# A hybrid GLA and Fourier encoder layer: exponentials behind an eviction, x in four pieces, gated state steps, gate loads by chunk

## The chip, the cores and the metric

The kernel runs on one core of one Trainium2 chip. The metric is the device time of one execution in microseconds; the time before is the median of three runs. A profiled execution gives the rows below. Engines are named as in the rows: PE is TensorE, DVE is VectorE, ACT is ScalarE, POOL is GpSimd, SP is SyncE, which issues nearly all DMAs.

## What is computed

One encoder layer in float32, 2048 positions by 1024 features:

```python
proj = x @ w_in                                  # q k v gates z_gla u z_fnet, 2592 wide
log_a = log_sigmoid(gate_lowrank @ w_up + b) / 16  # one per direction
o = gla_forward(q, k, v, log_af) + gla_backward(q, k, v, log_ab)   # 4 heads
y_gla = rmsnorm(o) * g * silu(z_gla)
y_fnet = (fft2(u, over positions and group features).real @ w_fnet) * silu(z_fnet)
y = concat(y_gla, y_fnet) @ w_out
out = layernorm(2 ** 0.25 * x + y) * ln_g + ln_b
```

`gla` is a scan: a state of 64x128 per head is decayed by exp(log_a) and receives k^T v at each position.

## The kernel before

Products keep nearly full float32 accuracy by splitting every operand into a rounded part ("hi", a copy by ScalarE at L55) and a remainder ("lo", a subtraction by DVE at L58); each product is three matmuls, hi*hi, hi*lo, lo*hi. The function `split` does both, so these two lines stand for many tiles (`xhl`, `bhl`, `et`, `yhl`, `mix`, `shl`, `wA_w`), and rows are told apart by tile.

The program has four phases. Phase 1 projects x to z_gla, u and z_fnet. Phase 2 merges two generators on TensorE: `qk_all`, which projects x to q and k in 8 blocks of 256 positions (L86, 96 matmuls a block), and `fnet_pe`, the Fourier part by groups g = 0 to 3: an FFT of 16 points over position blocks in DVE operations on `fw` (L522 to L534), its operands `bhl`, matmuls with the table `et` (`stage2`, L635), `yhl`, and `mixdown` (L655 into two buffers `pg`, a copy `qs`, and DVE's sum and difference L661 and L662). The first steps, the warm-up, are q and k blocks alone.

Phase 3 goes over 8 blocks of 256: projections pw and pv (L94), the gates' low-rank part (`gate_evac`, L781 to L783, evicts `rn`; `gate_t` transposes it at L813 and copies R at L814), the gate matmuls L825, `gates1` (scans L843 and L845), `gates2` with `middle` (L866 and the clip L867), and `gates3` (exponentials L872 and L873, `scaled` at L891 and L892, `alphas` L947 to L953). Each block also does the GLA chunks of the block before: `gla_s` and `gla_m` (scores L905, L906, transposes L909, masks L917, L918) and `gla_b` (the states' additions, L928, evicted to S by L930 and L932, and the inner part L935, evicted to `oi` by L939). GpSimd chains the states in `chain_step`: an addition L1194 and a multiplication with alpha L1197.

A handover (b = NBLK) does the last block's GLA part while the first output chunks start and the output weight is loaded; `find_range` checks the size of the exponents and writes a flag with a small matmul, L1063. Phase 4 goes over 16 chunks of 128 positions from 15 down to 0: `prep` (loads, a backward state step on GpSimd, the state matmul L1268, L1273, a square and its split), `norm` (L1282, L1283, scaling, and the multiplication with the gate z at L1289, on DVE for chunks 15 to 13 and on GpSimd below), `outp` (L1220, weights `wB` for the Fourier half and `wA` for the GLA half) and `finish` (residual, layer norm, store; L1299 to L1319).

Instructions are recorded in program order and then ordered by a scheduler of the language, engine by engine, by its own model of times. `tc.issue_after(ins)` adds one constraint: what is recorded inside stands behind `ins` wherever it runs on the engine of `ins`; `after(...)` in phase 3 joins several.

## Time and profile before

| | |
|---|---|
| time, median of 3 runs | 787.35 us (787.26 to 787.60) |
| profiled execution | 788.25 us, span of instructions 786.5 us |
| TensorE (PE) | 748.6 us busy, 95%, 5254 matmuls |
| DVE | 549.8 us, 70% |
| ScalarE (ACT) | 381.1 us, 48% |
| GpSimd (POOL) | 196.5 us, 25% |
| granted clock of TensorE, mean | 0.995 of full |
| DMA | 130.75 MB, mean 166 GB/s |

The profiled execution's span lies 1.75 us below its own time. "Idle before" in a row is the time for which the engine did nothing ahead of the instruction, with what released it. A row of the timeline can join several instructions (x4); a duration includes a pipeline's tail, so that starts of neighbours lie closer than durations.

### The profile page before, as it was taken

The numbers are of one execution on the slowest core, as the hardware profiler recorded it, in microseconds if no ns is written. First come the engines' busy times: TensorE is split into PE (matmuls) and PEld (weight loads), VectorE is DVE, ScalarE is ACT, GpSimd is POOL, SyncE is SP. The second block draws the span as 40 slices with busy tenths as digits, with TensorE's granted clock in tenths as the row PEclk, the third lists the DMA queues.
The fourth block names the chain that finished last, engine by engine and source line by source line (L and its number), as shares of the span: only waits on it lengthen the run. The fifth ranks groups of instructions, "written<-read, shape, count | busy, mean of one in ns | idle before, by whom it ended". The sixth has DMA issues, their size and how long they took to land.

```text
span 786.5 us, 13529 instructions
## 1 busy us (share of the span) xinstructions
PE 748.6 (95%) x5254; PEld 691.2 (88%) x5254; DVE 549.8 (70%) x808; ACT 381.1 (48%) x707; POOL 196.5 (25%) x137
## 2 busy tenths in 40 slices
PE   6999999999999998989999989999998999999995
PEld 5988899999999998989999888889876788888884
DVE  4693467464545789895748888888868777776764
ACT  6674372233223453445546777776655334334341
POOL 0000003020211000213310414444454454544531
PEclk9999999999999999999999999999999999999998
DMA  8876352444126974555775664555455454444222
GB/s 244 267 210 186 118 192 72 150 114 140 68 94 179 272 239 164 156 168 190 239 214 163 185 184 156 154 166 158 139 175 219 168 184 165 166 144 172 108 81 85
DMA packets 81935, 130.75 MB, mean 166 GB/s; under 512 B 7523, under 2 KB 55651, under 8 KB 81862
## 3 DMA queue, kind: packets, MB, share of 16 engines
q1 hardware_dynamic: 79558, 125.60, 50.5%
q10 hardware_dynamic: 2304, 4.20, 1.5%
q8 instruction: 43, 0.70, 0.4%
q14 instruction: 30, 0.25, 0.1%
HBM read 93.07 MB, written 36.70 MB: 165 GB/s over the span
## 4 chain that ended last, share of the span: by engine, by line
PE 55%; DVE 21%; ACT 11%; DMA 8%; issue 3%; SPq 1%; POOL 0%; DVEq 0%; ACTq 0%
PE mm L1220 17%; PE mm L374 17%; PE mm L86 4%; DMA xraw<-in_xt_dram 3%; DVE c L845 3%; PE mm L291 3%; PE mm L94 2%; DVE c L843 2%; ACT xhl L55 2%; DVE fw L534 2%; PE pa L635 2%; DMA fw<-u_d 2%; DVE fw L531 1%; PE pg L291 1%; PE pa L291 1%
## 5 line engine op out<-in xcount | busy, mean ns | idle before, releaser
L94 PE MATMUL mm<-wA_w,xhl 128*128 128x272 f32 x768 | 105.1, 292 | 0.0
L94 PEld LDWEIGHTS mm<-wA_w,xhl 128*128 128x128 f32 x768 | 98.6, 189 | 0.0
L86 PE MATMUL mm<-xhl,wC_w 128*128 128x256 f32 x768 | 96.0, 284 | 0.0
L86 PEld LDWEIGHTS mm<-xhl,wC_w 128*128 128x128 f32 x768 | 93.7, 192 | 0.5 <-issue 0.5
L1220 PE MATMUL mm<-wA_w,mix 128*128 128x512 f32 (+1 forms) x384 | 90.0, 384 | 1.5 <-ACT mix L55 1.1
L1220 PE MATMUL mm<-wB_w,mix 128*128 128x512 f32 (+1 forms) x384 | 89.3, 387 | 0.0
L1220 PEld LDWEIGHTS mm<-wA_w,mix 128*128 128x128 f32 x384 | 70.3, 188 | 16.6 <-ACT mix L55 1.5
L1194 POOL TENSOR_TENSOR S<-S 64x512 f32<-64x512 f32 x30 | 51.2, 1708 | 124.2 <-ACT S L930 121.2
L1220 PEld LDWEIGHTS mm<-wB_w,mix 128*128 128x128 f32 x384 | 69.5, 189 | 13.0
L58 DVE TENSOR_TENSOR xhl<-xraw,xhl 128x1024 fp32r<-128x1024 f32 (+1 forms) x52 | 57.5, 1111 | 29.8 <-ACT xhl L55 29.5
L55 ACT CAST xhl<-xraw 128x1024 fp32r<-128x1024 f32 (+1 forms) x52 | 49.3, 951 | 39.3 <-DMA xraw<-in_xt_dram 20.0
L55 ACT CAST x<-xraw 128x1024 fp32r<-128x1024 f32 x28 | 29.3, 1048 | 69.0 <-PE mm L374 54.9
L436 POOL TENSOR_TENSOR t<-t,t 128x512 f32<-128x512 f32 x7 | 10.9, 1557 | 190.4 <-ACT t L435 190.4
L1318 POOL TENSOR_TENSOR r<-r,lnb 128x1024 f32<-128x1024 f32 x15 | 35.7, 2383 | 89.5 <-issue 51.2
L58 DVE TENSOR_TENSOR x<-xraw,x 128x1024 fp32r<-128x1024 f32 x28 | 37.8, 1352 | 28.7 <-ACT x L55 28.7
L670 POOL TENSOR_TENSOR yf<-yf,zfl 128x256 f32<-128x256 f32 x24 | 20.9, 900 | 121.3 <-ACT yf L649 111.9
L1197 POOL TENSOR_TENSOR S<-S,alpha 64x512 f32<-64x512 f32 x30 | 48.6, 1620 | 2.4
L374 PE MATMUL mm<-wC_s,x 128*128 128x256 f32 x384 | 48.2, 283 | 0.0
L374 PEld LDWEIGHTS mm<-wC_s,x 128*128 128x128 f32 x384 | 47.1, 192 | 0.1
L291 PE MATMUL mm<-xhl,wA_w 128*128 128x512 f32 x192 | 43.9, 389 | 0.0
L291 PEld LDWEIGHTS mm<-xhl,wA_w 128*128 128x128 f32 x192 | 36.0, 188 | 7.4
L55 ACT CAST mix<-zg 128x512 fp32r<-128x512 f32 x15 | 9.3, 622 | 58.8 <-POOL zg L1289 56.0
(210 smaller groups left out, 1497.3 us busy)
## 6 DMA issues: line engine op xcount, KB each, us to landing
xraw<-in_xt_dram SPq DMA_DIRECT2D x48, 512.0 KB, 4.7
xr<-in_x_dram SPq DMA_DIRECT2D x16, 512.0 KB, 3.6
out_dram<-r SPq DMA_DIRECT2D x15, 512.0 KB, 2.7
xraw<-in_xt_dram SPq DMA_DIRECT2D x24, 256.0 KB, 4.7
zg_d<-zs SPq DMA_DIRECT2D x32, 128.0 KB, 3.7
u_d<-t SPq DMA_DIRECT2D x16, 256.0 KB, 3.2
zf_d<-t SPq DMA_DIRECT2D x16, 256.0 KB, 2.4
zfl<-zf_d SPq DMA_DIRECT2D x32, 128.0 KB, 3.4
```

The lines of the kernel that those rows point to most:

```text
L55: nc.scalar.copy(out=hi, in_=src)
L58: return (lo_eng or nc.vector).tensor_tensor(out=lo, in0=src, in1=f32(hi), op=ALU.subtract)
L86: mm = self.nc.tensor.matmul(ps, w[:, s, k, c0:c0 + P], x[:, m, k % 4, :], start=(k == 0 and i == 0), stop=(k == KB - 1 and i == 2))
L94: self.nc.tensor.matmul(ps, x[:, s, k % 4, t * P:(t + 1) * P], w[:, m, k, c0:c0 + cols], start=(k == 0 and i == 0), stop=(k == KB - 1 and ...
L291: nc.tensor.matmul(ps[c], self.wzg[:, s, 2 * q + kk, c * P:(c + 1) * P], x[:, m, kk], start=(q == 0 and kk == 0 and j == 0), stop=(q == 3 ...
L374: nc.tensor.matmul(ps[:, i], s_[s][:, k, i * P:(i + 1) * P], m_[m][:, k], start=(k == 0 and j == 0), stop=(k == 3 and j == 2))
L670: (nc.gpsimd if g < 3 else nc.vector).tensor_tensor(out=yb, in0=yb, in1=zf, op=ALU.mult)
L845: V.tensor_tensor_scan(out=c2[64:128, ::-1], data0=r2[64:128, ::-1], data1=g2[64:128, ::-1], initial=0.0, op0=ALU.mult, op1=ALU.add)
L1194: E.tensor_tensor(out=S[ds, dst], in0=S[ds, dst], in1=S[ds, src], op=ALU.add)
L1197: E.tensor_tensor(out=d3, in0=d3, in1=al, op=ALU.mult)
L1220: nc.tensor.matmul(y, c["mix"][:, s, eb], w[:, v, eb % 4, lo:lo + m], start=(ebs[0] == 4 and i == 0), stop=(ebs[0] == 0 and i == len(seq) ...
L1318: nc.gpsimd.tensor_tensor(out=r, in0=r, in1=lnb, op=ALU.add)
```

## The change

- `gates3` of blocks 3 to 7 is recorded inside `after(self.oi_ev)`, where `oi_ev` is the eviction L939.
- In `qk_all` x of the next block is still loaded in two halves, but split in four pieces of two feature blocks each, one after each of the four steps of a q and k block. The FFT's pieces (`nf`) after a `stage2` are held behind `mix_ev`, the subtraction of the last mixdown.
- The output weight is loaded by a new generator `wog_load`, its second half behind `oi_ev`; `find_range` moves from the handover into phase 4, after the first `norm`; the head of chunk 13 stands behind `at_ev` and `ks_ev`.
- A GpSimd copy `gate` of one element of chunk 15's `mix` is placed after the first `norm`; the state steps of chunks 13 to 10 are held behind it, those below behind the gate multiplication of the chunk three above, as before. Step 14 stays free.
- z of the gate is loaded by chunk (128 positions, two buffers) where it was by block (256, one buffer).
- In the last chunk DVE's L1306, whose result only other chunks use, is left out, and the second half of the store is issued by ScalarE.

```diff
@@ -659,7 +659,7 @@
                 nc.scalar.copy(out=qs[:, 0:n], in_=pq[0][:, 0:n])
                 k0 = ks[0]
                 nc.vector.tensor_tensor(out=yv[:, k0:k0 + n, :], in0=pq[1][:, 0:n], in1=qs[:, 0:n], op=ALU.add)
-                nc.vector.tensor_tensor(out=yv[:, 16 - k0:16 - k0 - n:-1, ::-1], in0=pq[1][:, 0:n],
+                self.mix_ev = nc.vector.tensor_tensor(out=yv[:, 16 - k0:16 - k0 - n:-1, ::-1], in0=pq[1][:, 0:n],
                                         in1=qs[:, 0:n], op=ALU.subtract)
 
             def gate_f(g, yf):
@@ -671,6 +671,8 @@
                     if b % 2:
                         bs = slice((b - 1) * BLK, (b + 1) * BLK)
                         nc.sync.dma_start(out=self.mf_d[:, g, bs], in_=yf[:, bs])
+
+            self.mix_ev = None
 
             def fnet_pe():
                 bt = bt0
@@ -690,7 +692,11 @@
                     for ks in ((1, 2), (3, 4), (5, 6), (7,), (0, 8)):
                         with self.tc.issue_after(self.qk_mm.ins):
                             yhl = stage2(g, bt, ks)
-                        next(nf, None)
+                        if self.mix_ev is None:
+                            next(nf, None)
+                        else:
+                            with self.tc.issue_after(self.mix_ev.ins):
+                                next(nf, None)
                         yield
                         if pend:
                             pend()
@@ -708,10 +714,19 @@
             def qk_all():
                 xn = self.x0
                 for b in range(NBLK):
-                    xh = xn
-                    if b + 1 < NBLK:
-                        xn = self.load_x(b + 1)
-                    yield from qk_block(b, xh)
+                    xh, xn, raws = xn, [], []
+                    for hf in range(2 if b + 1 < NBLK else 0):
+                        raw = self.xpool.tile([P, 4, BLK], F32, name="xraw", tag="xraw", bufs=2)
+                        nc.sync.dma_start(out=raw, in_=a["xt"][b + 1, :, 4 * hf:4 * hf + 4, :])
+                        raws.append(raw)
+                    for i, _ in enumerate(qk_block(b, xh)):
+                        yield
+                        if raws and i < 4:
+                            if i % 2 == 0:
+                                t = self.xpool.tile([P, 2, 4, BLK], F32R, name="xhl", tag="xhl", bufs=4)
+                                xn.append(t)
+                            t, js = xn[-1], slice(i % 2 * 2, i % 2 * 2 + 2)
+                            self.split(t[:, 0, js], t[:, 1, js], raws[i // 2][:, js])
 
             ga, gb = qk_all(), fnet_pe()
             def wvg_load():
@@ -976,7 +991,8 @@
                 if b > 1:
                     with after(self.ks_ev, self.at_ev):
                         gates2(b - 1, prev)
-                        gates3(b - 1, prev)
+                        with after(self.oi_ev):
+                            gates3(b - 1, prev)
                 if b > 2:
                     self.chain_f(2 * b - 3, 2 * b - 1)
                 qk_load(b, blk)
@@ -1040,13 +1056,15 @@
                 middle(prev, 1)
                 gates3(b - 1, prev, 1)
             with after(self.sc_ev, self.ks_ev):
-                self.wog = self.load_w("wA", a["w_out"][:, 0:4], 4, 1024)
+                wog = self.wog_load()
+                next(wog)
             self.outp(h14, [4, 5, 6, 7], (0,))
             gla_a(b - 1, 1, prev)
             gla_b(b - 1, 0, prev)
             nc.sync.dma_start(out=prev["oi"][:, 1].rearrange("p (h j) -> p h j", h=4), in_=self.zg_d[b - 1][:, :, P:2 * P])
             self.chain_f(2 * b - 1, 2 * b)
-            self.find_range(gp)
+            with after(self.oi_ev):
+                next(wog)
             gla_b(b - 1, 1, prev, True)
 
     def find_range(self, gp):
@@ -1076,6 +1094,15 @@
         self.head = {n: self.p4_head(n) for n in (NCH - 1, NCH - 2)}
         if not last:
             self.wog = self.load_w("wA", a["w_out"][:, 0:4], 4, 1024)
+
+    def wog_load(self):
+        w = self.wog = self.wpool.tile([P, 2, 4, 1024], F32R, name="wA_w", tag="wA")
+        for c in (0, 512):
+            for k in range(4):
+                raw = self.xpool.tile([P, 512], F32, name="wraw", tag="wraw", bufs=4)
+                self.nc.sync.dma_start(out=raw, in_=self.a["w_out"][:, k, c:c + 512])
+                self.split(w[:, 0, k, c:c + 512], w[:, 1, k, c:c + 512], raw)
+            yield
 
     def wof_load(self):
         nc = self.nc
@@ -1243,17 +1270,17 @@
                     self.p4_load(b)
                 d = self.blks[b]
                 fuse = n == NCH - 1 and "op" in d
-                if "zg" not in d:
-                    d["zg"] = p4.tile([P, 4, BLK], F32, name="zg4", tag="zg4", bufs=1)
-                    nc.sync.dma_start(out=d["zg"], in_=self.zg_d[b])
-                qp, oi, zg = d["q"][:, :, ts_], d["oi"][:, t], d["zg"][:, :, ts_]
+                qp, oi = d["q"][:, :, ts_], d["oi"][:, t]
+                if not fuse:
+                    zg = p4.tile([P, 4, P], F32, name="zg4", tag="zg4", bufs=2)
+                    nc.sync.dma_start(out=zg, in_=self.zg_d[b][:, :, ts_])
                 c = self.head.pop(n, None) or self.p4_head(n)
                 xr = p4.tile([P, DM], F32, name="xr", tag="xr", bufs=2)
                 nc.sync.dma_start(out=xr, in_=a["x"][n * P:(n + 1) * P, :])
                 if n < NCH - 1:
                     with ExitStack() as ia:
-                        if n + 3 in zgm and n + 3 < NCH - 1:
-                            ia.enter_context(self.tc.issue_after(zgm[n + 3].ins))
+                        if n < NCH - 2:
+                            ia.enter_context(self.tc.issue_after(zgm[min(n + 3, NCH) if n < NCH - 6 else NCH].ins))
                         self.chain_step(n, n + 1, n + 1, 1)
                 if fuse:
                     zg = oi.rearrange("p (h j) -> p h j", h=4)
@@ -1303,7 +1330,8 @@
                 V.bn_aggr(out=mv[:, 0:2], in_=st[:, 0:DM // w])
                 nc.scalar.activation(out=mv[:, 2:3], in_=mv[:, 1:2], func=AF.Ln, bias=e1[:, 1:2], scale=1.0)
                 nc.scalar.activation(out=mv[:, 2:3], in_=mv[:, 2:3], func=AF.Exp, scale=-0.5)
-                V.scalar_tensor_tensor(out=mv[:, 3:4], in0=mv[:, 0:1], scalar=-1.0, in1=mv[:, 2:3], op0=ALU.mult, op1=ALU.mult)
+                if n > 0:
+                    V.scalar_tensor_tensor(out=mv[:, 3:4], in0=mv[:, 0:1], scalar=-1.0, in1=mv[:, 2:3], op0=ALU.mult, op1=ALU.mult)
                 if n == 0:
                     for hf in range(2):
                         hs = slice(hf * 512, hf * 512 + 512)
@@ -1311,7 +1339,7 @@
                                                op0=ALU.subtract, op1=ALU.mult)
                         V.scalar_tensor_tensor(out=r[:, hs], in0=r[:, hs], scalar=mv[:, 2:3], in1=lnb[:, hs],
                                                op0=ALU.mult, op1=ALU.add)
-                        nc.sync.dma_start(out=a["out"][n * P:(n + 1) * P, hs], in_=r[:, hs])
+                        (nc.scalar if hf else nc.sync).dma_start(out=a["out"][n * P:(n + 1) * P, hs], in_=r[:, hs])
                     return
                 nc.scalar.activation(out=r, in_=r, func=AF.Identity, bias=mv[:, 3:4], scale=mv[:, 2:3])
                 V.tensor_tensor(out=r, in0=r, in1=lng, op=ALU.mult)
@@ -1324,9 +1352,17 @@
             self.outp(h14, [4, 5, 6, 7], (0, 1)[len(h14.get("y", ())):])
             cur = prep(NCH - 1)
             self.p4_load(NBLK - 2)
-            h13 = self.head[NCH - 3] = self.p4_head(NCH - 3)
+            with ExitStack() as es:
+                if "op" in self.blks[NBLK - 1]:
+                    es.enter_context(self.tc.issue_after(self.at_ev.ins))
+                    es.enter_context(self.tc.issue_after(self.ks_ev.ins))
+                h13 = self.head[NCH - 3] = self.p4_head(NCH - 3)
             self.outp(h13, [4, 5, 6, 7], (0,), get=self.pa)
             norm(cur)
+            gate = p4.tile([P, 1], F32, name="gate")
+            zgm[NCH] = nc.gpsimd.tensor_copy(out=gate, in_=f32(cur["mix"][:, 1, 3, 0:1]))
+            if "op" in self.blks[NBLK - 1]:
+                self.find_range(p4)
             for n in range(NCH - 1, -1, -1):
                 nxt = prep(n - 1) if n > 0 else None
                 if n == NCH - 3:
```

What moves is shown at three places; lines of the kernel after are 15 higher in phase 3, 27 in `chain_step` and below.

ScalarE, phase 3, an inner block (L872 and L873 are the exponentials, L930, L932 and L939 the evictions of `gla_b`, L781 and L782 the gate copies). Before:

```order
L872 ACTIVATE c<-g 128x1024
L781 CAST rn<-mm 128x32
L782 CAST rn<-mm 128x32
L873 ACTIVATE g<-g 128x1024
L930 COPY S<-pg 64x512
L797 COPY v<-mm 128x240
L932 COPY S<-pg 64x512
L939 COPY oi<-pg 128x512
L952 ACTIVATE alpha<-tf 64x8
L953 ACTIVATE alpha<-tf 64x8
L781 CAST rn<-mm 128x32
L782 CAST rn<-mm 128x32
```

After (L887 and L888 the exponentials, L945, L947, L954 the evictions, L796 and L797 the gate copies):

```order
L796 CAST rn<-mm 128x32
L797 CAST rn<-mm 128x32
L812 COPY v<-mm 128x240
L945 COPY S<-pg 64x512
L947 COPY S<-pg 64x512
L954 COPY oi<-pg 128x512
L887 ACTIVATE c<-g 128x1024
L967 ACTIVATE alpha<-tf 64x8
L968 ACTIVATE alpha<-tf 64x8
L888 ACTIVATE g<-g 128x1024
L796 CAST rn<-mm 128x32
L797 CAST rn<-mm 128x32
```

The evictions stand ahead of both exponentials, and the alphas between these.

DVE, FFT phase, warm-up (`xhl` the remainders of x, `bhl` those of the first FFT's operands). Before:

```order
L58 TENSOR_TENSOR xhl<-xraw,xhl 128x1024
L534 TENSOR_TENSOR fw<-fw 128x384
L531 SCALAR_TENSOR_TENSOR fw<-fw 128x128 x16
L58 TENSOR_TENSOR et<-eraw,et 128x384
L58 TENSOR_TENSOR bhl<-fw,bhl 128x512 x4
L58 TENSOR_TENSOR et<-eraw,et 128x384
L58 TENSOR_TENSOR xhl<-xraw,xhl 128x1024
```

After:

```order
L534 TENSOR_TENSOR fw<-fw 128x384 x2
L531 SCALAR_TENSOR_TENSOR fw<-fw 128x128 x8
L58 TENSOR_TENSOR xhl<-xraw,xhl 128x512
L531 SCALAR_TENSOR_TENSOR fw<-fw 128x128 x8
L58 TENSOR_TENSOR xhl<-xraw,xhl 128x512
L58 TENSOR_TENSOR bhl<-fw,bhl 128x512 x4
L58 TENSOR_TENSOR xhl<-xraw,xhl 128x512
L58 TENSOR_TENSOR et<-eraw,et 128x384 x2
L58 TENSOR_TENSOR xhl<-xraw,xhl 128x512
```

The pieces of block 1 stand around the FFT's operations, the last of them behind `bhl`; then come the pieces of block 2.

TensorE, handover (L1063 is `find_range`'s, L928 and L935 chunk 15's, L1268 the state matmuls, L1282 and L1283 the norm, `wB` and `wA` the output). Before:

```order
L1220 MATMUL mm<-wB_w,mix 128x512 x5
L1063 MATMUL pg<-fone,fm 1x1
L1220 MATMUL mm<-wB_w,mix 128x512 x2
L928 MATMUL pg<-v,ks 128x128 x4
L935 MATMUL pg<-at,v 128x128 x4
L1220 MATMUL mm<-wB_w,mix 128x512 x3
L1268 MATMUL pg<-qp,S 128x128 x4
L1220 MATMUL pa<-wB_w,mix 128x512 x12
L1282 MATMUL pg<-shl,ones 128x512
L1283 MATMUL pg<-shl,ones 128x512
L1268 MATMUL pa<-qp,S 128x128 x4
L1268 MATMUL pa<-qp_6658,S 128x128 x4
```

After (L1081 `find_range`'s, L943 and L950, L1295, L1309 and L1310, L1247 the output):

```order
L1247 MATMUL mm<-wB_w,mix 128x512 x2
L943 MATMUL pg<-v,ks 128x128 x4
L950 MATMUL pg<-at,v 128x128 x4
L1247 MATMUL mm<-wB_w,mix 128x512 x8
L1295 MATMUL pg<-qp,S 128x128 x4
L1247 MATMUL pa<-wB_w,mix 128x512 x12
L1309 MATMUL pg<-shl,ones 128x512
L1310 MATMUL pg<-shl,ones 128x512
L1081 MATMUL pg<-fone,fm 1x1
L1295 MATMUL pa<-qp,S 128x128 x4
L1309 MATMUL pg<-shl,ones 128x512
L1310 MATMUL pg<-shl,ones 128x512
```

`find_range`'s matmul stands behind the first norm, the second norm directly behind its state matmul, and chunk 13's state matmul behind 24 output matmuls.

## Rows read from the trace of the kernel before

**Rows 1.** Waits of TensorE over the whole span: us in total, times, longest us.

```profile
PE mm L813 <- DVE rn L783: 5.1, 6, 1.0
PE pg L655 <- DVE yf L662: 4.0, 4, 1.6
PE mm L825 <- ACT R L814: 2.7, 5, 0.8
PE pg L1063 <- ACT S L932: 1.6, 1, 1.6
PE pa L1220 <- ACT mix L55: 1.4, 1, 1.4
...
PE pg L655 <- DVE yhl L58: 0.8, 1, 0.8
```

**Rows 2.** TensorE's timeline, 505 to 511: start us, us, instruction, [idle before <-releaser].

```profile
506.96 0.32 PE L813 MATMUL mm<-ident,rn 128*96 128x128 f32 x1 [0.98 <-DVE rn L783]
...
509.27 0.74 PE L825 MATMUL mm<-R,wg 98*128 98x256 f32 x4 [0.49 <-ACT R L814]
```

**Rows 3.** Timeline of ScalarE, 499.8 to 509.6, same block.

```profile
501.96 1.06 ACT L872 ACTIVATE c<-g 128x1024 f32<-128x1024 f32 x1 [2.49 <-DVE g L867]
...
504.03 0.57 ACT L930 COPY S<-pg 64x512 f32<-64x512 f32 x1
```

**Rows 4.** Timeline of DVE, 499.8 to 509.6, same block.

```profile
501.18 0.69 DVE L867 TENSOR_SCALAR g<-g 128x1024 f32<-128x1024 f32 x1
...
504.30 1.22 DVE L892 TENSOR_TENSOR g<-kr,g 128x1024 f32<-128x1024 f32 x1
506.71 0.19 DVE L783 TENSOR_TENSOR rn<-mm,rn 128x32 fp32r<-128x32 f32 x1 [1.19 <-ACT rn L782]
```

**Rows 5.** TensorE by line, 262 to 298: busy us, mean ns | idle before.

```profile
L86 PE MATMUL mm<-xhl,wC_w 128*128 128x256 f32 x288 | 35.1, 284 | 0.0
```

**Rows 6.** Windows: us; busy us (instructions) of PE, PEld, DVE, ACT, POOL; clock; DMA.

```profile
262.50:297.50 35.00, 35.00 (x291) 34.76 (x290) 31.85 (x75) 15.87 (x25) 0.00 (x0) 1.00 0.83 253
297.50:400.00 102.50, 97.73 (x807) 96.77 (x806) 78.20 (x165) 45.20 (x82) 23.22 (x30) 1.00 0.57 180
```

**Rows 7.** Timeline of TensorE at the handover, 567 to 598.

```profile
568.73 0.37 PE L905 MATMUL pa<-qp,g 64*128 64x128 f32 x1 [0.80 <-DVE g L892]
...
580.00 0.19 PE L1063 MATMUL pg<-fone,fm 128*1 128x1 f32 x2 [1.60 <-ACT S L932]
...
589.42 1.05 PE L1268 MATMUL pa<-qp,S 128*128 128x128 f32 x8
...
592.57 0.50 PE L1282 MATMUL pg<-shl,ones 128*128 128x512 f32 x1
```

**Rows 8.** Windows of TensorE at the handover: us, busy us (instructions), granted clock.

```profile
580.90:585.00 4.10, 4.10 (x19) 0.58 0.00 2
590.50:598.00 7.50, 5.02 (x23) 1.00 0.54 212
```

**Rows 9.** Timeline of GpSimd, 499.8 to 507, the block of rows 2.

```profile
504.74 1.90 POOL L1194 TENSOR_TENSOR S<-S 64x512 f32<-64x512 f32 x1 [5.43 <-ACT S L930]
506.72 1.03 POOL L1197 TENSOR_TENSOR S<-S,alpha 64x512 f32<-64x512 f32 x1
```

**Rows 10.** Timeline of DVE, 603 to 613, gate of chunk 13.

```profile
608.93 2.45 DVE L1289 TENSOR_TENSOR zg<-o,zg 128x512 f32<-128x512 f32 x1 [0.70 <-DMA zg<-zg_d]
```

**Rows 11.** Timeline of DVE, 262 to 280, the warm-up of the FFT phase.

```profile
264.27 1.22 DVE L58 TENSOR_TENSOR xhl<-xraw,xhl 128x1024 fp32r<-128x1024 f32 x1
...
276.88 2.50 DVE L58 TENSOR_TENSOR bhl<-fw,bhl 128x512 fp32r<-128x512 f32 x4
279.29 0.56 DVE L58 TENSOR_TENSOR et<-eraw,et 128x384 fp32r<-128x384 f32 x1
```

**Rows 12.** Timeline of ScalarE, 577 to 598.5, a cast of the output weight.

```profile
577.73 0.62 ACT L55 CAST wA_w<-wraw 128x512 fp32r<-128x512 f32 x1 [1.69 <-DMA wraw<-in_w_out_dram]
```

**Rows 13.** Timeline, 774 to 787, the last chunk's normalisation on DVE.

```profile
779.07 0.15 DVE L1306 SCALAR_TENSOR_TENSOR mv<-mv 128x1 f32<-128x1 f32 x1
```

## The prediction

> **What bounds the kernel now.** I read the page first: TensorE is busy 748.6 of 786.5 us, so the only time to win is where it stands still or is clocked down. Then the waits of TensorE alone, grouped by line, since a gap there is a gap in the total [rows 1]: the transposes of the gate projections wait for DVE's remainder (L813, six times), the gate matmuls for the copy of R (L825), the FFT's mixdown for DVE's subtraction of the mixdown before or for a remainder of yhl (L655), and single waits stand at the handover from phase 3 to phase 4. Of the two ends of the program, the first loads and the last normalisation and store, the change touches only the second.
>
> Three places follow on the timelines.
>
> *Phase 3.* In one block of 256 positions TensorE waits 0.98 us for the second transpose and 0.49 us for R [rows 2]. The reason stands on ScalarE: after 2.49 us idle for the clip L867, it runs the exponential L872 at 501.96, the second (L873), and only then the evictions L930, L932, L939, the alphas and the second gate copies [rows 3]. DVE's remainder L783 of the second half then sits idle for these copies until 506.71 [rows 4].
>
> *FFT phase.* While the first three projection blocks run alone on TensorE, 288 matmuls take 35.1 us, so one every 0.1214 us [rows 5], and nothing is waited for: 35.00 of 35.00 us are busy. DVE is busy 31.85 of them, with remainders of x, the first FFT and the operands bhl. After that, to 400, TensorE is busy 97.73 of 102.50 us and DVE 78.20 [rows 6]; those 4.77 are the waits of L655.
>
> *Handover.* TensorE waits 0.80 us, then 1.60 [rows 7]. Behind the 1.60 the granted clock falls to the 1.2 GHz level: its mean is 0.58 over the 4.10 us to 585, so 0.42 x 4.10 = 1.7 us are lost. From 590.5 to 598 it is busy 5.02 of 7.50, so 2.5 are idle [rows 8].
>
> **The change part by part, in us gained.** The sum is made on the profiled execution: span 786.5, its own time 788.25, which is 0.90 above the median of 787.35; I carry the difference over to the median.
>
> *Exponentials behind L939 (blocks 3 to 7; block 2 is as before).* In the block shown the three evictions now fill the idle 2.49 us [rows 3]: 0.57 for each copy of S, and L939 about as long, which ends at about 502.2 because its matmul ends shortly before, so L872 starts 0.2 later, at 502.2, and L891 at 503.25. The alphas follow at once, L873 runs 503.6 to 504.65, the second gate copies end at 504.95 where they ended near 506.7. L892 can start at 504.65 and takes 1.22 [rows 4]; L783 is now behind it alone. That leaves a wait of about 0.1 for the transpose and none for R, since the two casts of x that stood ahead of the copy of R start 1.7 us earlier: 1.4 gained. But S is now ready early, so GpSimd's pair L1194 and L1197 comes into this stretch, where before it started at 504.74 [rows 9]. The first of the pair took 1.90 us there, while L892 ran, and the second, on as many numbers, 1.03 without it. L1197, which waits for the alpha at about 503.5, would start when L891 ends at 504.4 and hold L892 for its 1.03 us less the 0.25 in which L892 was not ready: L892 from 505.3 to 506.5, the transpose at about 506.7 in place of 506.96, and 0.25 + 0.49 = about 0.8 gained. I take 0.8 for three blocks, nothing for block 3 (there L867 comes late, so GpSimd is in before it), 0.4 for the last block with its other second half: **2.8**. Bounds: 1.4 in each block less a little, 6.5; and 0.3 lost in each if GpSimd also holds L867, about -1.5.
>
> The Trainium skill, page "SBUF — State Buffer", section "SBUF: two separate sides", speaks against this part: it says that DVE and GpSimd share one pair of SBUF ports, and that an instruction which has it keeps it to its end while the other is blocked altogether. By that rule the part is worth 0.8 a block, without it 1.4; the trace agrees with the rule at L1289, which took 2.45 us while GpSimd's L1318 ran [rows 10].
>
> *x in four pieces, FFT rows behind mix_ev.* What goes: the five waits of L655, 4.0 + 0.8 = 4.8 [rows 1, 6]. They came from FFT operations on 128x1024 and 128x512 that the scheduler had put between a mixdown's parts; now they stand behind the subtraction. What comes: a 128x1024 remainder of 1.22 us becomes two of 128x512, some 0.60 each as in bhl, 2.50 for four [rows 11], so DVE's work grows by next to nothing. But their places move: in the new order the fourth piece of block 1 stands behind all four bhl. From 264.27 to 279.29 [rows 11] DVE passed 15.02 us, of which two x remainders were 2.28, one et remainder 0.47 and idle time 0.93; the rest, 11.34, with four pieces of 0.60, ends at 278.0. TensorE started block 1 at 262.50 + 96 x 0.1214 = 274.15 and needs that piece at its 20th matmul, 276.46: a new stall of 1.6. For block 2 the last piece is cast on ScalarE behind an et whose raw load is issued late; between none and 1.6, I take 0.8. The first mixdown's yhl stands behind a piece of block 4: none to one piece, 0.5 with its cast. Later blocks have DVE idle a quarter of the time [rows 6]; nothing. Sum 4.8 - 1.6 - 0.8 - 0.5 = **1.9**, bounds 4.8 (pieces all in time) and -1.5 (the 1.6 stall clocks TensorE down as the 1.60 did, 1.7 [rows 7, 8], and each other one is at its end).
>
> *Handover.* The head of chunk 13 (two remainders of 0.60 after issue) and find_range's three small operations leave DVE's path to L892: the 0.80 goes. The 1.60 was a matmul of find_range, and it stood there because ScalarE's L930 and L932 were held behind a weight cast which had waited 1.69 us for its load [rows 12]; now the second half of wog_load follows L939, and about 0.2 stays: 1.4 gained, and the 1.7 of clock [rows 8]. The 2.5 behind 590.5 come from DVE and GpSimd alternating on chunks 15, 14 and 13; the copy `gate` holds GpSimd's steps from 13 on until chunk 15's mix is done: 2.5 gained. What is late next: chunk 14's norm now directly follows its own L1268, with a DVE add, a square, a cast and a remainder between them. Before, that chain took from 589.42 + 1.05 to 592.57, 2.1 [rows 7], and filled itself with other work; now it stands alone, with 0.5 more for the second half's remainder: 2.6 of new standing still. 0.8 + 1.4 + 1.7 + 2.5 - 2.6 = 3.8. As the new gap is longer than the 1.60 which was followed by the low clock, I expect the low clock again, -1.7: **2.1**. Bounds 5 (no drop and part of the chain covered) and 0.5.
>
> *Gate by chunks, two buffers.* L1289 of chunk 13 waited for the load of zg, issued only when its single buffer came free, then ran 2.45 [rows 10]; TensorE's 1.4 at L1220 [rows 1] hangs on it. With the half tile loaded early it goes: **1.4**, bounds 0 and 1.4. SyncE issues two loads of 256 KB for a block in place of one of 512 KB; phase 4 shows no wait of TensorE after it, and GpSimd's steps are placed as before, so nothing there.
>
> *Tail.* One DVE operation of 0.15 goes [rows 13], half of it hidden, and the last store's issue moves from SyncE to ScalarE, which has nothing left to do then: **0.1**. No row shows a last store issued by ScalarE; I bound it by two such operations either way, -0.3 and 0.3.
>
> Sum 2.8 + 1.9 + 2.1 + 1.4 + 0.1 = 8.3: 788.25 - 8.3 = 779.95 in a profiled execution, 787.35 - 8.3 = **779.0** by the median. A measurement of this kernel can tell some 0.2%, 1.6 us, from no change.
>
> **The rivals.**
> - *Better:* the new gap at the handover leaves the clock up (the 1.6 of L655 did: from 297.5 to 400 the granted clock is 1.00 [rows 1, 6]), +1.7, and L1197 does not fall on L892, +0.6 in four blocks: 774.9. Against it: GpSimd's work beside DVE's [rows 9, 10].
> - *GpSimd in front:* with S copied early, L1194 asks at about 501.2, where L867 starts at 501.18 [rows 4]. If it is in first, clip, exponentials and everything behind come some 1.2 late; the evictions ahead save nearly as much, each block loses 0.3, phase 3 gives -1.5 in place of 2.8, and the time is 783.3. The order of the two hangs on tenths.
> - *No net change:* the removed waits return one step later on DVE, the engine behind most of [rows 1], the FFT's 4.8 above all; what is left is inside 1.6 of 787.35. DVE's idle quarter speaks against it [rows 6].
> - *Slower:* a piece of x comes too late in block after block, each time 1.6 of stall and 1.7 of low clock, 3.3. All other parts and the 4.8 give 11.2, so it decides from the fourth of the seven loads on: 787.35 - 11.2 + 13.2 = 789.4, and more with each further one. For it: DVE is busy 91% of the warm-up [rows 6]. Against it: only three loads fall into that stretch.
>
> **How the numbers follow.** The forecast, 776 to 782 (its own bounds partly cancelling): 0.50. Better, 771 to 776: 0.17. GpSimd in front or the FFT part at its lower bound, 782 to 785.7: 0.17. No change 0.08, slower 0.08. So faster 0.84, same 0.08, slower 0.08. 773 to 785 leaves out the last two cases and the edges of two others, about 0.2.
>
> **What would show it.** In the changed trace: L813 waits of about 0.65 instead of 0.98 and no wait for R in blocks 4 to 6; L872 right behind L939; L892 starting behind a GpSimd L1197; a stall of TensorE of about 1.6 near 276.5 in a projection matmul, and no wait for L662; no wait at find_range's matmul, a gap of two parts near 586 to 588 with the clock at 0.50 behind it; no wait for chunk 13's mix. I am wrong if the stalls at pieces of x repeat after block 2, or if phase 3's blocks are not shorter.

## The result, and the profile after

The changed kernel takes 798.1 us (median of 4 runs, 793.87 to 799.96) where the kernel before took 787.48 beside it: the ratio is 1.0111, with a 95% interval of 1.0082 to 1.0141. It is slower by 10.6 us; the prediction said 8.3 us faster, with a range of 773 to 785.

TensorE's waits over the whole span of the changed kernel, in the columns of [rows 1]. In phase 3 and its helpers the lines are 15 higher than before, and 27 higher from `chain_step` on:

```profile
PE mm L828 <- DVE rn L798: 14.1, 6, 3.0
...
PE pg L1309 <- ACT shl L55: 2.1, 1, 2.1
...
PE pg L655 <- DVE yf L662: 1.4, 2, 1.1
PE pa L1247 <- ACT mix L55: 1.4, 1, 1.4
...
PE mm L86 <- DVE xhl L58: 1.2, 1, 1.2
...
PE mm L840 <- ACT R L829: 0.8, 1, 0.8
```

The transposes, here L828, which waited 5.1 us in all [rows 1], wait 14.1. The wait for R (L840) is down from 2.7 to the one of block 2, the FFT's from 4.8 to 1.4, and 1.2 is new in block 1 of the q and k projection; all of this is roughly as forecast. Two lines are not: the first, and the 1.4 for chunk 13's `mix` (L1247), which should have gone.

How long phase 3 lasts is read from the first and the last start of its projection matmuls L94 (line, count, shortest, median and longest duration in ns, first and last start). Before, then after:

```profile
L94 PE MATMUL mm<-wA_w,xhl x768: 282/288/376, 398.4 to 558.7; 128*128 128x272 f32 x192
```
```profile
L94 PE MATMUL mm<-wA_w,xhl x768: 282/288/576, 396.4 to 571.3; 128*128 128x272 f32 x192
```

160.3 us before, 174.9 after: phase 3 loses 14.6 us, which is the whole loss of 10.6 and 4 us that the other parts gained. Where these go shows in windows of TensorE over the phase, before and after (us, busy us, granted clock, DMA):

```profile
398.00:559.00 161.00, 150.96 (x1291) 1.00 0.59 176
```
```profile
396.00:571.00 175.00, 157.90 (x1286) 0.94 0.54 162
```

It stands still 17.1 us where it did 10.0, and for nearly the same number of matmuls it is busy 157.90 us where it was 150.96. So about half of the 14.6 is waiting, 7.1, and the other half, 6.9, is the same work at a lower granted clock, 0.94 in the mean.

One block of the changed kernel, the one that [rows 2 to 4] show of the kernel before. ScalarE, 502 to 516:

```profile
504.15 0.19 ACT L797 CAST rn<-mm 128x32 fp32r<-128x32 f32 x1
506.62 0.36 ACT L812 COPY v<-mm 128x240 f32<-128x240 f32 x1 [2.28 <-DVE rn L798]
506.88 0.58 ACT L945 COPY S<-pg 64x512 f32<-64x512 f32 x1
...
508.71 1.06 ACT L887 ACTIVATE c<-g 128x1024 f32<-128x1024 f32 x1
```

DVE over the same stretch:

```profile
504.12 1.20 DVE L881 TENSOR_TENSOR g<-c 128x1024 f32<-128x1024 f32 x1
...
505.35 0.70 DVE L882 TENSOR_SCALAR g<-g 128x1024 f32<-128x1024 f32 x1
...
506.20 0.16 DVE L966 TENSOR_TENSOR tf<-cend,cmid 64x8 f32<-64x8 f32 x1
506.40 0.19 DVE L798 TENSOR_TENSOR rn<-mm,rn 128x32 fp32r<-128x32 f32 x1
509.80 1.22 DVE L906 TENSOR_TENSOR qp<-qp,c 128x1024 f32<-128x1024 f32 x1 [3.21 <-ACT c L887]
511.21 1.79 DVE L907 TENSOR_TENSOR g<-kr,g 128x1024 f32<-128x1024 f32 x1 [0.19 <-DMA oi_d<-oi]
512.93 0.18 DVE L798 TENSOR_TENSOR rn<-mm,rn 128x32 fp32r<-128x32 f32 x1
```

TensorE, and its windows behind the wait:

```profile
510.18 0.27 PE L828 MATMUL mm<-ident,rn 128*96 128x128 f32 x1
513.16 0.32 PE L828 MATMUL mm<-ident,rn 128*96 128x128 f32 x1 [2.71 <-DVE rn L798]
513.23 2.42 PE L94 MATMUL mm<-wA_w,xhl 128*128 128x272 f32 x12
```
```profile
513.00:514.00 1.00, 0.84 (x7) 1.00 0.17 66
514.00:515.00 1.00, 1.00 (x6) 0.51 0.27 78
515.00:516.00 1.00, 1.00 (x6) 0.50 1.08 308
```

ScalarE has both gate copies done at 504.34 and then does nothing for 2.28 us. The next instruction in its order is L812, the copy of v from the same PSUM tile as the gate copies (`mm`, which the matmuls L94 write), and it waits for DVE's remainder L798. That tile is all that the two have in common, and both only read it. In the new order on DVE this remainder stands behind L881, the clip L882 and the alphas' sums, and is done at 506.59. Only then come the evictions L945 to L954, and behind these the exponential L887, at 508.71, 2.7 us after the clip was done. The second transpose waits 2.71 us in place of 0.98 [rows 2], and while the twelve matmuls behind it run, the granted clock falls to the 1.2 GHz level (0.51 and 0.50 from 514 on): they take 2.42 us where they took 1.76.

### The profile page after: what moved, and what is told of

Read it like the earlier page. It is cut to its first block, busy times and chain, and to the rows that moved or that the text cites. A ratio compares the mean times of both kernels' runs of the same rounds, so it can differ in the third digit from the quotient of the medians.

```text
span 797.3 us, 13555 instructions
## 1 busy us (share of the span) xinstructions
PE 756.1 (95%) x5254; PEld 700.2 (88%) x5254; DVE 554.5 (70%) x821; ACT 386.2 (48%) x721; POOL 199.8 (25%) x138
## 4 chain that ended last, share of the span: by engine, by line
PE 72%; DVE 12%; ACT 6%; DMA 4%; issue 3%; SPq 1%; DVEq 0%; ACTq 0%
PE mm L1247 20%; PE mm L374 20%; PE mm L86 9%; PE mm L291 5%; PE mm L94 3%; DVE c L860 3%; PE pa L635 3%; DVE c L858 2%; PE pa L1295 2%; PE pg L291 1%; PE pa L291 1%; PE pa L920 1%; PE mm L231 1%; DMA oi_d<-oi 1%; DVE g L853 1%
## 5 line engine op out<-in xcount | busy, mean ns | idle before, releaser
L94 PE MATMUL mm<-wA_w,xhl 128*128 128x272 f32 x768 | 109.4, 299 | 0.0
L94 PEld LDWEIGHTS mm<-wA_w,xhl 128*128 128x128 f32 x768 | 102.4, 196 | 0.0
L1247 PE MATMUL mm<-wA_w,mix 128*128 128x512 f32 (+1 forms) x384 | 91.2, 388 | 0.0
L1247 PE MATMUL mm<-wB_w,mix 128*128 128x512 f32 (+1 forms) x384 | 89.1, 387 | 0.0
L1247 PEld LDWEIGHTS mm<-wA_w,mix 128*128 128x128 f32 x384 | 71.6, 191 | 14.7
L1247 PEld LDWEIGHTS mm<-wB_w,mix 128*128 128x128 f32 x384 | 69.4, 188 | 13.0
L58 DVE TENSOR_TENSOR xhl<-xraw,xhl 128x1024 fp32r<-128x1024 f32 (+2 forms) x66 | 58.4, 901 | 30.8 <-ACT xhl L55 25.6
L1221 POOL TENSOR_TENSOR S<-S 64x512 f32<-64x512 f32 x30 | 45.8, 1526 | 132.3 <-ACT S L945 128.3
L55 ACT CAST xhl<-xraw 128x1024 fp32r<-128x1024 f32 (+2 forms) x66 | 50.7, 791 | 47.2 <-DMA xraw<-in_xt_dram 23.4
L1224 POOL TENSOR_TENSOR S<-S,alpha 64x512 f32<-64x512 f32 x30 | 53.9, 1798 | 7.6 <-ACT alpha L967 5.6
L670 POOL TENSOR_TENSOR yf<-yf,zfl 128x256 f32<-128x256 f32 x24 | 23.8, 1021 | 116.1 <-ACT yf L649 107.0
L374 PE MATMUL mm<-x,wB_s 128*128 128x256 f32 x288 | 36.3, 283 | 0.0
```

What stands on the lines that cost most here:

```text
L55: nc.scalar.copy(out=hi, in_=src)
L58: return (lo_eng or nc.vector).tensor_tensor(out=lo, in0=src, in1=f32(hi), op=ALU.subtract)
L94: self.nc.tensor.matmul(ps, x[:, s, k % 4, t * P:(t + 1) * P], w[:, m, k, c0:c0 + cols], start=(k == 0 and i == 0), stop=(k == KB - 1 and ...
L374: nc.tensor.matmul(ps[:, i], s_[s][:, k, i * P:(i + 1) * P], m_[m][:, k], start=(k == 0 and j == 0), stop=(k == 3 and j == 2))
L1221: E.tensor_tensor(out=S[ds, dst], in0=S[ds, dst], in1=S[ds, src], op=ALU.add)
L1224: E.tensor_tensor(out=d3, in0=d3, in1=al, op=ALU.mult)
```

## The experiments

My theory after this reading: the copy of v waits for the remainder, and the constraint put everything of ScalarE's block behind this copy. The rivals: the loss comes from the other parts; from GpSimd's state steps, now beside L907; or from L939 itself being late.

### The constraint taken off, and the constraint alone

```diff
                         gates2(b - 1, prev)
-                        with after(self.oi_ev):
-                            gates3(b - 1, prev)
+                        gates3(b - 1, prev)
```

> The changed kernel with the constraint behind L939's eviction taken off gates3, all else kept. Theory (in phase 3 ScalarE's copy of v, L812, waits for DVE's remainder L798 and now holds the evictions and with them the exponentials; each late transpose then costs clock too): phase 3 is as in the kernel before, L828 waits 5.1 in all, and the time is 787.4 less 2.0 of the FFT phase less some 2.7 from the handover on, 782.7. Rival (the loss is in the x pieces, the state steps or the handover): it stays near 798. Rival (the loss is shared): 788 to 794.

782.74 us (782.25 to 783.51), ratio 0.9923 (0.9903 to 0.9942) to the kernel before.

The kernel before with these lines added in place:

> The kernel before with that constraint alone added. Theory: phase 3 loses all of its 14.6 us, 787.4 + 14.6 = 802, with the granted clock below 0.9 behind each block's second transpose. Rival (the loss needs the other parts): within 2 us of 787.4.

801.2 us (800.37 to 802.68), ratio 1.016 (1.0137 to 1.0182). TensorE's waits and phase 3 in this kernel, then phase 3 of the one without the constraint:

```profile
PE mm L813 <- DVE rn L783: 14.1, 6, 3.0
```
```profile
L94 PE MATMUL mm<-wA_w,xhl x768: 282/289/575, 399.0 to 573.8; 128*128 128x272 f32 x192
```
```profile
L94 PE MATMUL mm<-wA_w,xhl x768: 282/288/376, 394.8 to 555.1; 128*128 128x272 f32 x192
```

The one line makes the whole loss: phase 3 takes 174.8 us with it and 160.3 without, and the wait is the 14.1 us of the changed kernel to the tenth. All other parts together are a gain of 0.8%, and the time is the theory's.

### The copy of v ahead of the remainder

```diff
                 nc.scalar.copy(out=v[:, 272:512], in_=pw[:, 0:240])
+                V.tensor_tensor(out=rn[:, t, 32:64].bitcast(F32R), in0=pw[:, 240:272], in1=rn[:, t, 0:32], op=ALU.subtract)
```

and the same subtraction taken out of `gate_evac`, where it stood ahead of the copy. The changed kernel with this exchange is called the mended kernel below.

> The changed kernel with the copy of v recorded ahead of the remainder of rn, so that L812 no longer waits for L798; the computation is the same. Theory: the copy of v and the evictions run 2.3 us earlier, the wait of the second transpose falls from 2.7 to between 0.1 and 0.7, no clock drop, no wait for R, so that phase 3 is 0.8 to 1.4 a block shorter than before: 778 to 781. Rival (GpSimd's state steps, now beside L907, are what makes the transposes late): the waits stay above 1.5 and the time above 790. Rival (the exponentials are late because L939's own matmul is): the wait stays near 1.0 with a wait for R near 0.5, 783.

779.6 us (778.79 to 780.4), ratio 0.9876 (0.9857 to 0.9895). The mended kernel's phase 3, then ScalarE and the clip on DVE in the block shown above:

```profile
L94 PE MATMUL mm<-wA_w,xhl x768: 282/288/377, 396.9 to 553.5; 128*128 128x272 f32 x192
```
```profile
496.62 0.38 ACT L811 COPY v<-mm 128x240 f32<-128x240 f32 x1
497.35 0.58 ACT L946 COPY S<-pg 64x512 f32<-64x512 f32 x1 [0.35 <-PE pg L944]
...
499.18 1.06 ACT L888 ACTIVATE c<-g 128x1024 f32<-128x1024 f32 x1
```
```profile
497.89 0.69 DVE L883 TENSOR_SCALAR g<-g 128x1024 f32<-128x1024 f32 x1
```

Phase 3 takes 156.6 us, 3.7 less than before and 18.3 less than in the changed kernel, and the clock of its windows is 1.00. That settles it: with the order of two recorded instructions exchanged, the copy of v (L811) waits for nothing, the evictions start at 497.35, ahead of the clip's end at 498.6, and the exponential follows L955's eviction. The remainder, now recorded behind the copy, loses nothing: DVE's trace has no idle time put down to waiting in front of it. In the inner blocks a second transpose follows the last one after 20.7 us, where the kernel before took 21.6. Most of the wait that is left comes from GpSimd, as the next section shows; the second transpose, then DVE and GpSimd of that block:

```profile
503.63 0.31 PE L829 MATMUL mm<-ident,rn 128*96 128x128 f32 x1 [0.79 <-DVE rn L813]
```
```profile
501.68 1.79 DVE L908 TENSOR_TENSOR g<-kr,g 128x1024 f32<-128x1024 f32 x1 [0.19 <-DMA oi_d<-oi]
```
```profile
500.48 1.92 POOL L1225 TENSOR_TENSOR S<-S,alpha 64x512 f32<-64x512 f32 x1 [0.74 <-ACT alpha L968]
```

The remainder product takes 1.79 us beside the multiplication L1225, against 1.22 [rows 4]. The wait is 0.79, close to the 0.65 of the prediction's working with the lock.

In block 3, the first with the constraint, GpSimd's addition L1222 also comes in front of the clip. GpSimd, DVE and the second transpose there:

```profile
455.46 1.64 POOL L1222 TENSOR_TENSOR S<-S 64x512 f32<-64x512 f32 x1 [4.31 <-ACT S L946]
```
```profile
455.87 1.25 DVE L963 TENSOR_TENSOR cend<-cend,cmid 128x8 f32<-128x8 f32 x1
457.05 0.68 DVE L883 TENSOR_SCALAR g<-g 128x1024 f32<-128x1024 f32 x1
```
```profile
462.27 0.32 PE L829 MATMUL mm<-ident,rn 128*96 128x128 f32 x1 [1.52 <-DVE rn L813]
```

A sum for the alphas takes 1.25 us where it took 0.16 in the kernel before, the clip starts that much later, and the wait of this block is 1.52 where it was 1.01 there.

### The state steps out of the way

First both forward steps of a block held behind the remainder product by a GpSimd copy of one element, then the first step's multiplication alone:

```diff
                 if b > 2:
-                    self.chain_f(2 * b - 3, 2 * b - 1)
+                    gt = gp.tile([P, 1], F32, name="gt", tag="gt", bufs=2)
+                    ge = nc.gpsimd.tensor_copy(out=gt, in_=prev["ek"][:, 0, 0:1])
+                    with after(ge):
+                        self.chain_f(2 * b - 3, 2 * b - 1)
```

> As the run above, and GpSimd's forward state steps of a block are held, by a copy of one element on GpSimd, until the remainder product L892 of the block is done. Theory: L907 no longer shares its time with a state step (1.22 in place of 1.8), the transpose's wait falls to about 0.1, 0.6 a block less than the run above: 776 to 778.5. Rival (the lock costs nothing there): the same time as the run above. Rival (both steps now meet the remainders of x or the scans and delay R): 1 to 5 us above the run above.

787.6 us (784.2 to 791.03), ratio 0.9986 (0.9964 to 1.0007), against 779.6 of the mended kernel in the same comparison: 3 us more than the worse rival allowed.

```diff
-        E.tensor_tensor(out=d3, in0=d3, in1=al, op=ALU.mult)
+        with ExitStack() as es:
+            if hold:
+                es.enter_context(self.tc.issue_after(hold().ins))
+            E.tensor_tensor(out=d3, in0=d3, in1=al, op=ALU.mult)
```

> The mended kernel, with only the multiplication of the first of a block's two forward state steps held on GpSimd until the remainder product of the block (L907 of the changed kernel, here one line lower) is done; the addition ahead of it and the second step stay. Theory (the transposes' wait of 0.8 is that multiplication's 1.9 us on the shared ports): the wait falls to about 0.2, 0.6 in each of four or five blocks, 776.6 to 777.5. Rival (the multiplication then holds up the remainders of x and the masks behind them as both steps did): 779.6 to 784, with a wait at the inner matmuls L951.

784.41 us (783.07 to 784.62), ratio 0.9929 (0.9909 to 0.995). TensorE's waits in the second, DVE in a block of the first, then a window of TensorE in the first and in the second:

```profile
PE pg L951 <- DVE at L934: 7.3, 5, 1.7
...
PE mm L829 <- DVE rn L813: 0.9, 4, 0.2
```
```profile
458.50 3.45 DVE L58 TENSOR_TENSOR xhl<-xraw,xhl 128x1024 fp32r<-128x1024 f32 x2
461.88 3.22 DVE L1125 TENSOR_TENSOR wB_w<-wraw,wB_w 128x512 fp32r<-128x512 f32 x2
```
```profile
460.00:480.00 20.00, 18.09 (x149) 0.91 0.50 148
```
```profile
460.00:480.00 20.00, 18.30 (x163) 1.00 0.53 163
```

The transposes' wait for the remainder is gone (0.9 in all), and 7.3 us of waits stand one step later, at the inner matmuls L951, because the steps now meet the remainders of x and of the output weight: 3.45 and 3.22 us where the mended kernel has 2.35 and 1.28 for the same two pairs. My theory for these runs fell, the rival's wait came as written. The two runs differ by the clock: with both steps held, waits of 1.9 us at L951 were each followed by the low clock, so that phase 3 lost 9.5 us; with the multiplication alone held, waits of 1.7 were not, and it lost 3.0. The 0.8 us at the transpose is the cheaper place for this work.

### The reordering alone

```diff
-                V.tensor_tensor(out=rn[:, t, 32:64].bitcast(F32R), in0=sl, in1=rn[:, t, 0:32], op=ALU.subtract)
...
                 nc.scalar.copy(out=v[:, 272:512], in_=pw[:, 0:240])
+                V.tensor_tensor(out=rn[:, t, 32:64].bitcast(F32R), in0=pw[:, 240:272], in1=rn[:, t, 0:32], op=ALU.subtract)
```

> The kernel before with the copy of v recorded ahead of the remainder of rn, and nothing else. The scheduler then places the evictions ahead of the second exponential by itself. Theory (that wait, and not the place of the exponentials, is what stands in phase 3's way): the phase gains about 3 of its 7 us of waits, 784 to 785. Rival (the wait was free in the kernel before, hidden behind the exponentials): 787.4, no change.

790.44 us (788.37 to 795.51), ratio 1.0017 (0.9993 to 1.0041): no difference. Phase 3 takes 161.3 us, and the transposes' waits are 8.6 in all. Without the constraint the scheduler leaves the first exponential ahead of the evictions and puts the second behind them, which again delays the remainder product. So the rival's time came, though not by its reason: the waits did not stay as they were, they rose from 5.1 to 8.6. And neither half gains alone: without the reordering the constraint loses 14.5 us of phase 3, without the constraint the reordering gains nothing, and together they gain 3.7 in phase 3.

### The FFT part

The kernel before with the change's first four hunks, x in four pieces and the FFT's rows behind `mix_ev`:

```diff
-                        next(nf, None)
+                        if self.mix_ev is None:
+                            next(nf, None)
+                        else:
+                            with self.tc.issue_after(self.mix_ev.ins):
+                                next(nf, None)
...
+                            self.split(t[:, 0, js], t[:, 1, js], raws[i // 2][:, js])
```

> The kernel before with the FFT part alone: x in four pieces and the FFT's rows behind the mixdown's subtraction. Theory: the part is worth what the changed trace shows between the first q and k matmul and the start of phase 3, 2.0 to 2.7, with a new stall of 1.2 to 1.6 in block 1's matmuls and one or two of L655 left: 785 to 785.8. Rival (a stall there drops the clock): 787 or more.

786.31 us (784.4 to 787.04), ratio 0.9957 (0.9942 to 0.9971), beside a kernel before that took 789.58 there. That is 3.3 us gained (2.3 to 4.6 by the interval), more than the theory's 1.6 to 2.4.

The mended kernel with x in halves again, the FFT's rows still held:

```diff
-                    xh, xn, raws = xn, [], []
...
+                    xh = xn
+                    if b + 1 < NBLK:
+                        xn = self.load_x(b + 1)
+                    yield from qk_block(b, xh)
```

> The mended kernel (copy of v ahead of the remainder), with x split in halves as in the kernel before; the FFT's rows stay behind the mixdown's subtraction. Theory A (the pieces only bring the stall of 1.2 to 1.4 in block 1, the gain is that of the FFT's rows): 1.3 less than the mended kernel's 779.6, 778.3. Theory B (a whole remainder of 1.22 us between two mixdowns makes L655 wait, so the pieces are needed): 781 to 784. The same 779.6 would say that the pieces cancel out.

780.31 us (779.83 to 781.98), ratio 0.9881 (0.986 to 0.99), against 0.9876 of the mended kernel. TensorE's window in the first, with the new stall, then the one larger wait in the second, with the projection matmuls that follow it:

```profile
255.00:400.00 145.00, 142.19 (x1170) 1.00 0.66 207
```
```profile
278.68 21.02 PE L86 MATMUL mm<-xhl,wC_w 128*128 128x256 f32 x173 [0.84 <-DVE xhl L58]
```
```profile
366.90 0.62 PE L655 MATMUL pg<-yhl,wcs 128*128 128x256 f32 x3 [2.21 <-DVE yf L662]
...
368.16 4.42 PE L86 MATMUL mm<-xhl,wC_w 128*128 128x256 f32 x24
```

In the first 2.81 us stand still where 4.77 did, 1.96 gained; the stall at block 1's fourth piece is 0.84 here and 1.19 in the changed kernel, and no clock fell. The stall is no fixed price: of the ten traces with pieces, nine have 0.8 to 1.4 and the one without the constraint has none. With x in halves that stall is gone and a wait of 2.21 stands where 1.1 to 1.3 stood with pieces, followed by the low clock: 24 matmuls take 4.42 us where such a group takes 3.04 elsewhere. The times of the two kernels do not differ beyond their intervals, so the pieces about cancel out, and it is the FFT's rows that gain.

### The end: chunk 13, the last store, the gap at the norm

The addition of lnb for chunk 15 held on GpSimd behind chunk 13's gate multiplication:

```diff
-                nc.gpsimd.tensor_tensor(out=r, in0=r, in1=lnb, op=ALU.add)
-                nc.sync.dma_start(out=a["out"][n * P:(n + 1) * P, :], in_=r)
+                def add():
+                    nc.gpsimd.tensor_tensor(out=r, in0=r, in1=lnb, op=ALU.add)
+                    nc.sync.dma_start(out=a["out"][n * P:(n + 1) * P, :], in_=r)
+                if n == NCH - 1:
+                    return add
+                add()
...
+                if n == NCH - 2:
+                    g2 = nc.gpsimd.tensor_copy(out=gate2, in_=f32(nxt["mix"][:, 1, 3, 0:1]))
+                    with self.tc.issue_after(g2.ins):
+                        late()
```

> The mended kernel, with the addition of lnb and the store of chunk 15 moved on GpSimd behind the gate multiplication of chunk 13. Theory (the wait of 1.37 for chunk 13's mix is left because DVE's L1315 takes 2.45 beside that addition, not because of the load of the gate): the wait goes, 778.2. Rival (the load or something else is late as well): the wait stays near 1.4 and the time at 779.6. Rival (the addition then meets chunk 12's work): a new wait further on, 779.6 to 782.

779.7 us (778.62 to 779.99), ratio 0.9871 (0.9851 to 0.9891). In the changed kernel the wait of 1.4 for chunk 13's mix is still there. The rows of TensorE, DVE and GpSimd; L1314 is the operation ahead of the gate multiplication, which itself now takes 0.67:

```profile
622.45 3.03 PE L1247 MATMUL pa<-wA_w,mix 128*128 128x512 f32 x12 [1.37 <-ACT mix L55]
```
```profile
618.10 2.45 DVE L1314 TENSOR_TENSOR o<-o,sq 128x512 f32<-128x512 f32 x1
```
```profile
617.62 2.39 POOL L1346 TENSOR_TENSOR r<-r,lnb 128x1024 f32<-128x1024 f32 x1 [2.69 <-issue]
```

And in this run, the next wait:

```profile
606.01 0.50 PE L1311 MATMUL pg<-shl,ones 128*128 128x512 f32 x1 [0.90 <-DVE shl L58]
```

The 1.37 is gone, so it was DVE's 2.45 beside GpSimd's addition and not the load of the gate. But 0.90 came back at the next norm, where a remainder of `shl` now takes 2.87 us beside that addition: the last of the cases written ahead. In the profiled execution the clock fell behind the gap at chunk 14's norm (0.59 from 584 to 588), ahead of the work that was moved; it fell there in six of the eight traces with this gap of 2.1, not in the mended kernel's and in the next run's. The time is the same.

The last store's second half from SyncE again:

```diff
-                        (nc.scalar if hf else nc.sync).dma_start(out=a["out"][n * P:(n + 1) * P, hs], in_=r[:, hs])
+                        nc.sync.dma_start(out=a["out"][n * P:(n + 1) * P, hs], in_=r[:, hs])
```

> The mended kernel with both halves of the last store issued by SyncE again. From the last chunk's aggregate L1303 to the end of the span, the kernel before and two kernels with its tail took 8.4, seven with the changed tail 9.1 to 9.4. Theory (SyncE waits at the end for ScalarE's later store): 0.8 less, 778.8, and 8.3 to 8.4 in that stretch. Rival (the stretch varies with something else): 779.6.

779.57 us (778.48 to 781.19), ratio 0.9868 (0.9833 to 0.9902): no difference to 779.6, and the stretch from the aggregate to the end is 9.3 us, not 8.4. The theory fell.

Ten of chunk 14's matmuls put into the gap ahead of its norm, on top of that run; then with the late addition as well:

```diff
-            self.outp(h14, [4, 5, 6, 7], (0, 1)[len(h14.get("y", ())):])
...
                 nxt = prep(n - 1) if n > 0 else None
+                if n == NCH - 1 and len(rest) == 1:
+                    self.outp(h14, [4, 5, 6, 7], rest)
```

> The run above, and the second half of chunk 14's Fourier product (12 matmuls) recorded behind chunk 14's state matmul, so that 10 of them stand in front of chunk 14's norm where TensorE waited 2.09. Theory: that wait goes and no low clock follows it, 1.5 to 2 less than the run above, 777. Rival (the norm's chain on DVE and ScalarE, not TensorE, sets the end of the handover): the waits return at chunk 15's mix or at chunk 13's norm, within 0.5 of the run above.

779.54 us (778.52 to 780.43), ratio 0.9871 (0.9841 to 0.9902): the rival's time.

> The run above with the addition of lnb of chunk 15 behind chunk 13's gate multiplication as in the run on that. Theory (alone its 1.37 came back as 0.90 at the next norm and as another clock): 0.5 to 1.4 less than the run above, 776. Rival (what is gained at one norm is lost at the next): the same as the run above.

778.66 us (777.63 to 779.09), ratio 0.9852 (0.9821 to 0.9883). In both runs the gap's 2.09 went. In the first, two waits of 0.8 for GpSimd's state steps are new in the handover, and in the second one; the 1.6 at chunk 13's norm in both was 1.4 in the mended kernel. This last kernel is the fastest in the study, 1.5% under the kernel before, but its interval covers the mended kernel's; the three edits of this section together are worth at most a microsecond.

## Why the prediction was wrong

**The step that failed** is the first of phase 3's: "the three evictions now fill the idle 2.49 us", and with it that L872 starts "0.2 later". I had the new order of ScalarE before me, with the copy of v between the gate copies and the first eviction, and gave it neither a time nor a wait. It waits for DVE's remainder: in the block shown L887 starts 2.7 us behind the clip, not some 0.3. The kernel before shows that wait, in the rows for L797, and the changed kernel for L812 (idle time of ScalarE before the line, and how often):

```profile
  DVE rn L783: 6.9, 4
```
```profile
  DVE rn L798: 19.5, 10
```

In the block of [rows 3] it cost nothing, because both exponentials stood ahead of the copy and L783 ran in between. The change took that cover away: the gate copies and the copy of v now come while DVE is still at the clip, the remainder stands behind the clip and the sums for the alphas, and everything on ScalarE that was to fill the idle time stands behind the copy. Costing an order without asking of each instruction what it waits for gave 2.8 us gained in place of 14.6 lost. The clock was not in this part's sum either, and it made half of the loss. The exchange of the two instructions fits the rest of that walk: with the wait away, an inner block gains 0.9 where 0.8 was forecast, and phase 3 gains 3.7. Why the language lets one reader of a tile wait for another, no run shows.

**The lock** was right: 1.79 for the product beside GpSimd's multiplication and a wait of 0.79 where I had put about 0.65. The Trainium skill's rule of the shared ports ("SBUF — State Buffer", "SBUF: two separate sides") agrees with these rows, and with L1314's 2.45 beside GpSimd's addition. GpSimd in front of the clip was not what happened in the changed kernel: in the block shown the step came at 507.6, after it. With the copy's wait away it did happen, in block 3: the clip came 1.1 us late there, for the rival's 1.2. In blocks 4 to 7 it was a sum for the alphas behind the clip that took 1.26 us, so the order did hang on tenths.

**The FFT part** was right in size: 1.9 predicted, 1.96 by the idle time of the part alone, 3.3 by the times of that run. The stall came at the matmul that was named, with 0.8 to 1.4 in nine traces and nothing in one, for 1.6, and without the clock's fall that I kept as a bound.

**The handover and the gate loads**, 2.1 + 1.4. No run has these parts alone, so they are read from the traces. From the last L94 to the last chunk's aggregate (the end of its statistics, L1303 before) the kernel before takes 219.4 us, the changed one 216.7: 2.7 gained for 3.5. The 0.80 and the 1.60 went, the gap at chunk 14's norm came as written, 2.10 and 0.2, and behind it the low clock:

```profile
601.81 0.50 PE L1309 MATMUL pg<-shl,ones 128*128 128x512 f32 x1 [2.10 <-ACT shl L55]
```
```profile
603.00:606.00 3.00, 3.00 (x9) 0.50 0.93 298
```

The 1.4 of the gate by chunks is the term that failed: I took the load for the cause where my own row [rows 10] had both, the load and DVE's 2.45 beside GpSimd. The load was early now, the collision stayed, one operation further ahead. A wait of 0.9 at chunk 15's own norm is new, and in no sum of mine.

**The tail** was put at 0.1 gained and lost 0.9: 8.4 us from the aggregate to the end of the span in four profiles with the old tail became 9.1 to 9.4 in seven with the new one. The three kernels that gave the store back to SyncE took 9.3, 8.6 and 9.0, so ScalarE's issue is not shown to be the cause. What lengthens the stretch stays open; giving the store back changed the time by nothing (779.57 against 779.6).

**The rivals.** The one on the slower side had the kind of loss right and the place wrong: a stall in block after block with a low clock behind each, about 2.5 us a block here where I had 3.3, but from the copy of v and not from the pieces of x. A chance of 0.08 for slower was too small for a change that moves eight instructions on an engine whose waits I had not each looked up.

## What to carry to other kernels

When an order moves, list for every instruction ahead of the one that matters what it waits for, also those that look harmless: a wait that costs nothing where it stands is still in the program, and whatever covered it may be what the change moves. Here two engines read one tile, and the order in which the reads were recorded decided who waited for whom: ScalarE stood idle 19.5 us in 10 cases with DVE's read recorded first, and neither engine waited with ScalarE's first. So look at that order, and let the reader come first whose engine has work waiting behind it. A gain at the bound of TensorE is not safe until the clock behind the new waits is counted: here half of the loss was the same work at a lower clock.

## What the runs showed of the hardware

- The waits of 2.7 to 3.1 us ahead of the transposes in the changed kernel were each followed by the low clock: 0.50 in the block shown, and means of 0.54 to 0.87 in windows of 4 to 10 us around the others. Of the shorter ones, those of 1.9 at the inner matmuls were followed by it (both state steps held) and those of 1.7 at the same place were not (one multiplication held). The gap of 2.1 at chunk 14's norm was followed by it in six traces of eight, and in the mended kernel's the clock stayed at 1.00 behind it. The length of the wait alone didn't decide it.
- Work of GpSimd that is moved away from one DVE operation is paid by another: the two pairs of remainders took 6.7 us in place of 3.6 when both state steps stood beside them, and with chunk 15's addition moved off L1314 (2.45 us), a remainder of `shl` took 2.87.
